# Transposed attention blocks through DRAM, keys permuted, and the product with v one point later

## The chip, the cores and the metric

The kernel runs on one core of a Trainium2 chip. A core has a matrix engine (TensorE; PE in the profile, with its weight loads shown apart as PEld), VectorE (DVE), ScalarE (ACT), GpSimd (POOL) and SyncE (SP), which here issues nearly all the DMAs. Each engine works through its own instructions in order; semaphores tie the engines and the DMAs together. The metric is the device time of one execution in microseconds: the median of three runs before was 1619.12 us (1618.91 to 1619.42). The profiled execution took 1619.76 us, of which the profile's span is 1618.0 us.

## The reference, cut to what matters

One layer of an encoder is computed for two sequences of 512 tokens, width 1024: a state-space branch, a differential attention, a cross attention to 256 memory tokens, a gated merge of the three, and a gated feed-forward network. The change touches the differential attention alone. It has 4 heads with two maps of 64 query and key columns each, and values 128 wide:

```
s = jnp.einsum('bqhd,bkhd->bhqk', qblk, k).astype(jnp.float32) * scale
probs = jax.nn.softmax(s, axis=-1).reshape(Bn, DIFF_HEADS, 2, Q_BLOCK, L)
w = probs[:, :, 0] - lam * probs[:, :, 1]
return jnp.einsum('bhqk,bkhe->bqhe', w.astype(v.dtype), v)
```

The sum over the keys in the last line does not depend on the order in which the keys are numbered, as long as w and v number them alike.

## The kernel before, in words

All large products are made in three passes: each float32 operand is split into a rounded part and a rest (`split`, lines 132 to 139: ScalarE copies the rounded part, line 134, and VectorE subtracts, line 135), and TensorE multiplies high by high, high by low and low by high. Weights arrive by DMA as `wf` (line 146) and are split to `wh` and `wl`. A projection (`units`) makes one output bank of 512 columns, `bkmm`, out of 24 products.

The differential attention runs over 16 pairs of query blocks: 4 heads, 2 sequences, 2 pairs of 128 queries. A pair u goes through five steps.

- `scores(2u)`: TensorE makes the score banks `bksc` of two query blocks (128 queries by 512 keys, two maps). VectorE takes the row maxima (line 858), ScalarE the exponentials (lines 861 and 862), VectorE the reciprocals and the combination of the two maps (lines 864 to 866), and VectorE transposes the result in blocks of 32 by 32 into the tile `eT` (line 867). `eT` has one buffer.
- The same function then issues 16 DMAs on SP's queue (line 872). Each takes 32 partitions of `eT` to 32 partitions of the tile `pL`, so that keys stand on the partitions and queries in the free dimension. One run of bytes in them is 64 floats.
- `turn(u)`: ScalarE copies the rounded part of `pL` into `pH`, VectorE puts the rest into `pL`. The two tiles come from one pool of four slots.
- `outputs(u)`: TensorE multiplies with the values, 12 products of 256 columns into the bank `bkoo` ("the product with v" below). After the second pair of a head and sequence ScalarE copies the bank out (line 899).
- `squares` and `normed`: the norm over the head, and a DMA of the result to DRAM (line 919), where the last of the three merges fetches it.

The values come from `v_units`, with x as the stationary operand (128 tokens by 128 columns, loaded into TensorE) and 256 weight columns moving over it: 384 such products in all, half of them during the cross attention and half during this stage. Keys and queries come from `qk_units`, through `rotated`.

Between these steps `fill` hands TensorE projections from a list (keys and queries of the next heads, values, gates, then the merges). A step of the loop has two such fillings. On TensorE the order written down is kept. On the other engines and on SP's queue a scheduler has ordered the instructions at build time, from estimated times.

Of the kernel before, what the change touches and what calls it, by code (L numbers as in the profile page):

```python
# [10 lines left out]
F32 = mybir.dt.float32  # L11
F32R = mybir.dt.float32r
# [7 lines left out]
P = 128  # L20
L = 512
DM = 1024
KD = DM // P
# [49 lines left out]
def encoder(ctx: ExitStack, tc: tile.TileContext, a, out):  # L73
# [14 lines left out]
    def open_tags(es, side=None, **tags):  # L88

        for tag, n in tags.items():  # L90
            pools[tag] = es.enter_context(tc.tile_pool(name=tag, bufs=n, side=side, reuse_waits="tile"))
# [14 lines left out]
    def slot(tag, shape=(P, NT), dt=F32, name="sl"):  # L106
        return pools[tag].tile(list(shape), dt, tag=tag, name=name)
# [23 lines left out]
    def split(hi, lo, src, scale=None):  # L131

        if scale is None:
            h = S.copy(hi, src)  # L134
            l_ = V.tensor_tensor(out=lo, in0=src, in1=hi.bitcast(F32), op=ALU.subtract)  # L135
        else:
            h = S.activation(out=hi, in_=src, func=AF.Copy, scale=scale)
            l_ = V.scalar_tensor_tensor(out=lo, in0=src, scalar=scale, in1=hi.bitcast(F32), op0=ALU.mult, op1=ALU.subtract)
        return h, l_
# [456 lines left out]
    def fill(n):  # L596
        nonlocal owed
        owed += n
        while owed > 0 and queue:
            r = next(queue[0], None)  # L600
            if r is None:
                queue.pop(0)
            else:
                owed -= r
        if not queue:
            owed = 0
# [28 lines left out]
    def v_units(hf, res):  # L635

        ws = [weight(a["w_v"][hf, c]) for c in range(2)]
        for s in range(NS):
            vh, vl = (slot("v2" if hf == 1 and s == 0 else "v", [P, 4, 256], F32R, n_) for n_ in ("vh", "vl"))
            for i2 in range(2):  # L640
                ob = bank()
                for kt in range(KD):
                    wh, wl = ws[kt // 4]
                    wsl = slice(kt % 4 * 256, kt % 4 * 256 + 256)
                    for i in range(2):
                        dst = ob[:, i * 256 : i * 256 + 256]
                        tk = slice(s * L + (2 * i2 + i) * P, s * L + (2 * i2 + i + 1) * P)
                        PE.matmul(dst, xh[kt][:, tk], wh[:, wsl], start=(kt == 0 and i == 0), stop=False)
                        PE.matmul(dst, xh[kt][:, tk], wl[:, wsl], start=False, stop=False)
                        PE.matmul(dst, xl[kt][:, tk], wh[:, wsl], start=False, stop=(kt == KD - 1 and i == 1))  # L650
                    if kt == KD - 1:
                        split(*(v_[:, 2 * i2 : 2 * i2 + 2, :].rearrange("p t n -> p (t n)") for v_ in (vh, vl)), ob)
                    if kt % 2 == 1:
                        yield 6
            res.append((vh, vl))
# [76 lines left out]


    open_banks(mm=2, sc=2, tr=1, oo=1)
    open_tags(phase, v2=2, qk=12, pT=4)
    aes = ExitStack()
    ap_ = aes.enter_context(tc.tile_pool(name="att", bufs=2, reuse_waits="tile"))
    acol = aes.enter_context(tc.tile_pool(name="acol", bufs=2, reuse_waits="tile"))
# [5 lines left out]
    def rotated(is_q):  # L744

        hl = tuple(slot("qk", [P, NT], F32R, n_) for n_ in ("rh", "rl"))

        def use(s, o):
            cs = slice(s * L, (s + 1) * L)
            t1 = ap_.tile([P, L], F32, tag="t1", name="t1", bufs=1)  # L750
            V.tensor_tensor(out=t1, in0=o, in1=rope[0], op=ALU.mult)
            t2 = ap_.tile([P, L], F32, tag="t2", name="t2", bufs=1)
            V.stream_shuffle(t2, o, mask)  # L753
            PO.tensor_tensor(out=t2, in0=t2, in1=rope[1], op=ALU.mult)  # L754
            PO.tensor_tensor(out=t1, in0=t1, in1=t2, op=ALU.add)
            split(hl[0][:, cs], hl[1][:, cs], t1, scale=0.125 if is_q else None)

        return hl, use

# [76 lines left out]
              gate_units(), merges()]  # L836
    s0, ss, osb = {}, {}, {}
    pl, ods = {}, {}

    def scores(i):  # L840
        nonlocal last_e
        h, s, qt = steps[i]
        cs = slice(s * L, (s + 1) * L)
        if h and s == qt == 0:
            finish(dk[h])
        if qt == 0:
            s0[h, s] = acol.tile([P, 4], F32, tag="s0", name="s0", bufs=3)
        (qh, ql), (kh, kl) = qk[h, True], qk[h, False]
        sc = [pools["sc"].tile([P, 2, L], F32, tag="sc", name="bksc") for _ in range(2)]
        for t in range(2):  # L850
            qs_ = slice(s * L + (qt + t) * P, s * L + (qt + t + 1) * P)
            for q_, k_ in ((qh, kh), (qh, kl), (ql, kh)):
                for mp, rows in enumerate(MAPS):
                    PE.matmul(sc[t][:, mp], q_[rows, qs_], k_[rows, cs], start=(k_ is kh and q_ is qh), stop=(q_ is ql))
        eT = ap_.tile([P, 16, 2, 32], F32, tag="eT", name="eT", bufs=1)
        for t in range(2):
            nb = acol.tile([P, 2], F32, tag="dnb", name="nb")
            V.tensor_reduce(out=nb, in_=sc[t], axis=AX.X, op=ALU.max, negate=True)
            e0, e1 = (ap_.tile([P, L], F32, tag=f"d{mp}e", name="e", bufs=2 - mp) for mp in range(2))
            sm0, sm1 = s0[h, s][:, qt + t : qt + t + 1], acol.tile([P, 1], F32, tag="ds", name="sm")  # L860
            S.activation(out=e0, in_=sc[t][:, 0], func=AF.Exp, bias=nb[:, 0:1], accum_out=sm0)
            last_x = S.activation(out=e1, in_=sc[t][:, 1], func=AF.Exp, bias=nb[:, 1:2], accum_out=sm1)
            r1 = acol.tile([P, 1], F32, tag="dr", name="r")
            V.reciprocal(r1, sm1)
            V.scalar_tensor_tensor(out=r1, in0=r1, scalar=nlam, in1=sm0, op0=ALU.mult, op1=ALU.mult)
            V.scalar_tensor_tensor(out=e0, in0=e1, scalar=r1, in1=e0, op0=ALU.mult, op1=ALU.add)
            last_e = last_x, V.transpose(eT[:, :, t, :], e0)
        raw = pl[i // 2] = slot("pT", [P, 4, 2 * P], F32R, "pL")
        rows = eT.rearrange("p (j c) t q -> p j c (t q)", c=4)
        for g in range(4):  # L870
            for c in range(4):
                nc.sync.dma_start(raw.bitcast(F32)[32 * c : 32 * c + 32, :, 64 * g : 64 * g + 64], rows[32 * g : 32 * g + 32, :, c])

    def turn(u):
        lo, hi = pl[u], slot("pT", [P, 4, 2 * P], F32R, "pH")
        split(hi, lo, lo.bitcast(F32))
        pT[u] = hi, lo

    def outputs(u):

        h, s, qt = steps[2 * u]
        if h == 2 and s == 0:
            finish(v1_)
        vh, vl = (v1 if h >= 2 else v0)[s]
        vs = slice((h % 2) * P, (h % 2) * P + P)
        pH, pL = pT.pop(u)
        if qt == 0:
            ods[h, s] = bank("oo")
            osb[h, s] = rp.tile([P, L], F32, tag="nsq", name="osb", bufs=2)
        cs = slice(qt * P, (qt + 2) * P)  # L890
        od = ods[h, s][:, cs]
        for j in range(4):
            PE.matmul(od, vh[:, j, vs], pH[:, j, :], start=(j == qt == 0), stop=False)
            PE.matmul(od, vh[:, j, vs], pL[:, j, :], start=False, stop=False)
            PE.matmul(od, vl[:, j, vs], pH[:, j, :], start=False, stop=(j == 3 and qt == 2))
        if qt == 2:
            for a_ in range(2):
                cs = slice(a_ * 2 * P, (a_ + 1) * 2 * P)
                S.copy(osb[h, s][:, cs].rearrange("p (t g q) -> p g t q", t=2, q=32),
                       ods[h, s][:, cs].rearrange("p (g t q) -> p g t q", t=2, q=32))  # L900
# [18 lines left out]
        nc.sync.dma_start(bD[1, h, :, s * L : (s + 1) * L], osb[h, s])  # L919

    n, first = len(steps), {}
    for i in range(-1, n + 3):
        if i % 2 and i + 1 < n:
            scores(i + 1)
        fill(10 if i < n - 1 else 16)
        if i % 2 and 0 < i <= n:
            turn(i // 2)
        fill(10)
        if i % 2 == 0 and 0 < i <= n:
            outputs(i // 2 - 1)  # L930
        if 1 < i <= n + 1 and steps[i - 2][2] == 3:
            squares(i - 2)
        if i > 2 and steps[i - 3][2] == 3:
            normed(i - 3)
        if i in (17, 19, 21, 23):
            t = (0, 1, 3, 2)[(i - 17) // 2]
            with yielding(last_e):
                merge_split(b0, 0, t, "v" if t == 3 else "qk", first[t])
        if i in (15, 17, 19, 21):
            t = (0, 1, 3, 2)[(i - 15) // 2]  # L940
            first[t] = merge_load(0, t)
# [927 lines left out]
```

## Time and profile before

| | |
|---|---|
| median of three runs | 1619.12 us (1618.91 to 1619.42) |
| profiled execution | 1619.76 us, span 1618.0 us |
| TensorE busy | 1575.7 us, 97% of the span |
| VectorE, ScalarE, GpSimd busy | 74%, 39%, 34% |
| TensorE busy from 519 to 783 us (differential attention) | 233.62 of 264 us, granted clock 0.94 |

The profile's busy time of TensorE includes time in which it works at a lower clock: a row's PEclk says which share of full speed was granted. Matrix products overlap in the records: one of 512 columns is shown as 0.39 us long, while the next one starts 0.23 us after it. Idle time is therefore counted only from the shown end of the one before.

### The profile page before, as it was taken

Reading aid. Unit: us, or ns where it says so; the run is one execution under the profiler, and the core shown is the slowest. Engines: PE = TensorE matmul, PEld = TensorE weight load, DVE = VectorE, ACT = ScalarE, POOL = GpSimd, SP = SyncE. Lnnn points to the kernel's source line nnn. Section 1 sums busy time; section 2 is a strip of 40 time slices with the busy share of each in tenths; the row PEclk is TensorE's granted clock in tenths of the full one; section 3 lists DMA queues with packets and bytes.
Section 4 is the critical chain, followed back from the end, with each engine's and each line's share of the span. In section 5 each row is a group of like instructions: output and inputs, shape, how many; then the busy total and the mean of one; then the engine's idle time right before and its main releaser. Section 6 shows DMA issues by size and latency. Waiting matters only on the chain. (4 is left out here: it accounts for less than half of the span.)

```text
span 1618.0 us, 21693 instructions
## 1 busy us (share of the span) xinstructions
PE 1575.7 (97%) x7706; PEld 1312.5 (81%) x7706; DVE 1190.4 (74%) x1843; ACT 632.8 (39%) x1107; POOL 552.2 (34%) x434
## 2 busy tenths in 40 slices
PE   9999999999999899888999999999999999999998
PEld 7888888888898678677788888888888888888877
DVE  7978994076764777767545659888898887988874
ACT  6544223175552346455223444233333323323323
POOL 0010000001322211210144344777677554435673
PEclk9999999999999999999999999999999999999999
DMA  9554533685762232235653542323333223785512
GB/s 356 188 165 141 174 118 124 188 279 186 249 227 85 57 120 56 77 96 183 215 177 104 161 139 65 115 95 124 130 117 121 108 92 127 287 313 197 169 59 105
DMA packets 142540, 246.26 MB, mean 152 GB/s; under 512 B 50528, under 2 KB 82272, under 8 KB 142432
## 3 DMA queue, kind: packets, MB, share of 16 engines
q1 hardware_dynamic: 141856, 244.46, 45.3%
q8 instruction: 61, 1.00, 0.3%
q14 instruction: 47, 0.39, 0.1%
q10 hardware_dynamic: 576, 0.41, 0.1%
HBM read 165.16 MB, written 71.27 MB: 146 GB/s over the span
## 5 line engine op out<-in xcount | busy, mean ns | idle before, releaser
L66 PE MATMUL bkmm<-xh,wh 128*128 128x512 f32 x640 | 253.3, 396 | 0.0
L66 PE MATMUL bkmm<-xh,wl 128*128 128x512 f32 x640 | 250.4, 391 | 0.0
L66 PE MATMUL bkmm<-xl,wh 128*128 128x512 f32 x640 | 249.9, 391 | 0.0
L66 PE MATMUL bkmm<-tl,wh 128*128 128x512 f32 (+1 forms) x621 | 241.1, 388 | 0.0
L66 PE MATMUL bkmm<-th,wl 128*128 128x512 f32 (+1 forms) x621 | 240.7, 388 | 0.0
L66 PE MATMUL bkmm<-th,wh 128*128 128x512 f32 (+1 forms) x621 | 240.7, 388 | 0.0
L134 ACT CAST wh<-wf 128x1024 fp32r<-128x1024 f32 (+2 forms) x134 | 117.5, 877 | 259.6 <-PE bkmm L66 174.0
L135 DVE TENSOR_TENSOR wl<-wf,wh 128x1024 fp32r<-128x1024 f32 (+2 forms) x134 | 148.3, 1106 | 62.5 <-ACT wh L134 57.8
L66 PEld LDWEIGHTS bkmm<-xh,wh 128*128 128x128 f32 x640 | 120.3, 188 | 27.5 <-issue 4.4
L66 PE MATMUL bkmm<-th,w 128*128 128x512 f32 x432 | 140.6, 391 | 1.8 <-DVE nsq L1128 1.2
L66 PEld LDWEIGHTS bkmm<-xh,wl 128*128 128x128 f32 x640 | 120.2, 188 | 25.7 <-issue 0.4
L66 PEld LDWEIGHTS bkmm<-xl,wh 128*128 128x128 f32 x640 | 120.3, 188 | 22.9
L66 PEld LDWEIGHTS bkmm<-th,wh 128*128 128x128 f32 x621 | 116.6, 188 | 24.0
L66 PEld LDWEIGHTS bkmm<-tl,wh 128*128 128x128 f32 x621 | 116.6, 188 | 24.0
L66 PEld LDWEIGHTS bkmm<-th,wl 128*128 128x128 f32 x621 | 116.5, 188 | 23.9 <-DVE wl L135 0.2
L1191 POOL TENSOR_TENSOR up<-up,acc 128x512 f32<-128x512 f32 x44 | 83.7, 1920 | 90.5 <-DVE up L1128 86.8
L452 POOL TENSOR_TENSOR raw<-raw 128x128 f32<-128x128 f32 x28 | 14.7, 524 | 288.8 <-DVE nb L543 231.9
L66 PEld LDWEIGHTS bkmm<-th,w 128*128 128x128 f32 x432 | 80.9, 188 | 21.9 <-DVE nsq L1128 2.1
L793 POOL TENSOR_TENSOR mg<-mg,gl 128x1024 f32<-128x1024 f32 x16 | 43.8, 2737 | 145.8 <-DVE gl L789 141.1
L66 PE MATMUL bkmm<-tl,w 128*128 128x512 f32 x216 | 84.1, 389 | 0.0
L134 ACT CAST wh<-ws 128x1024 fp32r<-128x1024 f32 x44 | 46.3, 1053 | 89.2 <-PE bkmm L66 58.0
L754 POOL TENSOR_TENSOR t<-t,rs 128x512 f32<-128x512 f32 x16 | 26.3, 1645 | 160.1 <-DVE t L753 111.2
(661 smaller groups left out, 3596.5 us busy)
## 6 DMA issues: line engine op xcount, KB each, us to landing
wf<-in_w_in SPq DMA_DIRECT2D x40, 512.0 KB, 3.9
wD<-hl SPq DMA_DIRECT2D x28, 512.0 KB, 2.9
w<-wD SPq DMA_DIRECT2D x28, 512.0 KB, 4.8
gD<-gt SPq DMA_DIRECT2D x24, 512.0 KB, 3.0
gl<-gD SPq DMA_DIRECT2D x24, 512.0 KB, 4.1
wf<-in_w_fg SPq DMA_DIRECT2D x22, 512.0 KB, 3.5
wf<-in_w_fu SPq DMA_DIRECT2D x22, 512.0 KB, 3.5
aD<-ac SPq DMA_DIRECT2D x22, 512.0 KB, 2.8
```

Of the source, the lines that this page charges most:

```text
L66: return self.put(self.eng.matmul(*args, **kw))
L134: h = S.copy(hi, src)
L135: l_ = V.tensor_tensor(out=lo, in0=src, in1=hi.bitcast(F32), op=ALU.subtract)
L452: PO.tensor_tensor(out=a22, in0=a21, in1=a22, op=ALU.add)
L754: PO.tensor_tensor(out=t2, in0=t2, in1=rope[1], op=ALU.mult)
L793: PO.tensor_tensor(out=mg[m], in0=mg[m], in1=gt, op=ALU.add)
L1191: PO.tensor_tensor(out=up, in0=up, in1=accs[s], op=ALU.mult)
```

## The change

The 16 DMAs of a pair are replaced by four stores of 32 partitions each from `eT` to a DRAM tile `eD`, and one load of 128 partitions from there to `pL`. One run of bytes is now 256 floats. In `eD`, and so in `pL`, a partition holds every fourth key of a block of 128. Two other places are numbered to match: `rotated` writes the split keys with the columns of each block of 128 permuted (it reads its source at a step of four floats), and `v_units` takes as its stationary operand every fourth token, a step of four floats, in place of 128 tokens side by side. `turn` and `outputs` see `pL` and `pH` in the arrangement that the load leaves. `pL` gets three slots and `pH` one, in place of four for both. In the loop, `outputs(u)` moves from the end of one step to after the first filling of the next, ahead of the `turn` of the pair after it; `squares` and `normed` move back by one step too. No arithmetic is added or removed.

```diff
@@ v_units
-                        tk = slice(s * L + (2 * i2 + i) * P, s * L + (2 * i2 + i + 1) * P)
-                        PE.matmul(dst, xh[kt][:, tk], wh[:, wsl], start=(kt == 0 and i == 0), stop=False)
-                        PE.matmul(dst, xh[kt][:, tk], wl[:, wsl], start=False, stop=False)
-                        PE.matmul(dst, xl[kt][:, tk], wh[:, wsl], start=False, stop=(kt == KD - 1 and i == 1))
+                        xh_, xl_ = (x_[kt][:, s * L + 2 * i2 + i : (s + 1) * L : 4] for x_ in (xh, xl))
+                        PE.matmul(dst, xh_, wh[:, wsl], start=(kt == 0 and i == 0), stop=False)
+                        PE.matmul(dst, xh_, wl[:, wsl], start=False, stop=False)
+                        PE.matmul(dst, xl_, wh[:, wsl], start=False, stop=(kt == KD - 1 and i == 1))
@@
-    open_tags(phase, v2=2, qk=12, pT=4)
+    open_tags(phase, v2=2, qk=12, pL=3, pH=1)
@@ rotated
-            split(hl[0][:, cs], hl[1][:, cs], t1, scale=0.125 if is_q else None)
+            if is_q:
+                split(hl[0][:, cs], hl[1][:, cs], t1, scale=0.125)
+            else:
+                split(*(t_[:, cs].rearrange("p (c j k) -> p c j k", c=4, j=4) for t_ in hl), t1.rearrange("p (c k j) -> p c j k", c=4, j=4))
@@
+    eD = drp.tile([16, 4, 4, 32, 2 * P], F32, name="eD")
@@ scores
-        raw = pl[i // 2] = slot("pT", [P, 4, 2 * P], F32R, "pL")
-        rows = eT.rearrange("p (j c) t q -> p j c (t q)", c=4)
         for g in range(4):
-            for c in range(4):
-                nc.sync.dma_start(raw.bitcast(F32)[32 * c : 32 * c + 32, :, 64 * g : 64 * g + 64], rows[32 * g : 32 * g + 32, :, c])
+            nc.sync.dma_start(eD[i // 2, g].rearrange("c k n -> k c n"),
+                              eT[32 * g : 32 * g + 32].rearrange("k (c j) t q -> k c (j t q)", c=4))
+        pl[i // 2] = slot("pL", [P, 4, 2 * P], F32R, "pL")
+        nc.sync.dma_start(pl[i // 2].bitcast(F32), eD[i // 2].rearrange("g c k n -> (c k) g n"))
@@ turn
-        lo, hi = pl[u], slot("pT", [P, 4, 2 * P], F32R, "pH")
+        lo, hi = pl[u], slot("pH", [P, 4, 2 * P], F32R, "pH")
         split(hi, lo, lo.bitcast(F32))
-        pT[u] = hi, lo
+        pT[u] = tuple(t_.rearrange("p g (j n) -> p j g n", j=4) for t_ in (hi, lo))
@@ the loop over the steps
-    for i in range(-1, n + 3):
+    for i in range(-1, n + 4):
         if i % 2 and i + 1 < n:
             scores(i + 1)
         fill(10 if i < n - 1 else 16)
+        if i % 2 and 2 < i <= n + 1:
+            outputs(i // 2 - 1)
         if i % 2 and 0 < i <= n:
             turn(i // 2)
         fill(10)
-        if i % 2 == 0 and 0 < i <= n:
-            outputs(i // 2 - 1)
-        if 1 < i <= n + 1 and steps[i - 2][2] == 3:
-            squares(i - 2)
-        if i > 2 and steps[i - 3][2] == 3:
-            normed(i - 3)
+        if 2 < i <= n + 2 and steps[i - 3][2] == 3:
+            squares(i - 3)
+        if i > 3 and steps[i - 4][2] == 3:
+            normed(i - 4)
```

How the order moves is seen best on two engines. On SP's queue, in the middle of the stage, where the last projections of keys and queries load their weights (`wf<-in_w_in`), stood before:

```order
L872 DMA pL<-eT 32x4x64 x16
L919 DMA bD<-osb 128x512
L146 DMA wf<-in_w_in 128x1024
L872 DMA pL<-eT 32x4x64 x32
L919 DMA bD<-osb 128x512
L146 DMA wf<-in_w_in 128x1024 x2
L872 DMA pL<-eT 32x4x64 x32
L919 DMA bD<-osb 128x512
L146 DMA wf<-in_w_up 128x512
```

At the same place now stands (lines 872 to 876 are the new DMAs, and line 919 has become 923):

```order
L873 DMA eD<-eT 32x4x256 x4
L923 DMA bD<-osb 128x512
L876 DMA pL<-eD 128x4x256
L873 DMA eD<-eT 32x4x256 x4
L876 DMA pL<-eD 128x4x256
L146 DMA wf<-in_w_in 128x1024
L923 DMA bD<-osb 128x512
L146 DMA wf<-in_w_in 128x1024
L873 DMA eD<-eT 32x4x256 x4
L876 DMA pL<-eD 128x4x256
```

A pair has five DMAs on the queue in place of 16, and one of them, the load, waits for the four stores ahead of it; a weight load can stand right behind it.

On TensorE, at the first product with v, stood before (`bkoo` is the product's bank, `bksc` that of the scores, which `x2` marks as two products on halves of the rows):

```order
L66 MATMUL bkoo<-pH,vh 128x256
L66 MATMUL bkoo<-pL,vh 128x256
L66 MATMUL bkoo<-pH,vl 128x256
L66 MATMUL bksc<-rh 128x512 x2
L66 MATMUL bksc<-rl,rh 128x512 x2
L66 MATMUL bksc<-rh,rl 128x512 x2
```

and now:

```order
L66 MATMUL bksc<-rh,rl 128x512 x2
L66 MATMUL bkmm<-xh_127,wh 128x512
L66 MATMUL bkmm<-xl_135,wh 128x512
L66 MATMUL bkmm<-xh_127,wl 128x512
L66 MATMUL bkmm<-xh_128,wh 128x512
L66 MATMUL bkmm<-xl_136,wh 128x512
L66 MATMUL bkmm<-xh_128,wl 128x512
L66 MATMUL bkoo<-pH,vh 128x256
L66 MATMUL bkoo<-pL,vh 128x256
L66 MATMUL bkoo<-pH,vl 128x256
```

The product has moved behind the next pair's scores and one filling of 6 (elsewhere 12) projections.

## The prediction

> **What bounds the kernel now.** First the page's busy shares, then the span cut into stretches, since a mean over the whole says little.
>
> ```profile
> span 1618.0 us, 21693 instructions
> PE 1575.7 (97%) x7706; PEld 1312.5 (81%) x7706; DVE 1190.4 (74%) x1843; ACT 632.8 (39%) x1107; POOL 552.2 (34%) x434
> ...
> 519.00:783.00 264.00, 233.62 (x1236) 191.06 (x1234) 188.48 (x297) 127.80 (x285) 39.14 (x24) 0.94 0.35 107
> 783.00:1618.00 835.00, 825.75 (x3754) 684.88 (x3752) 635.55 (x746) 269.79 (x378) 461.24 (x324) 1.00 0.42 142
> ```
>
> TensorE is the bound. The columns of the last two rows are PE, PEld, DVE, ACT, POOL, granted clock, DMA share and GB/s. Nearly all that TensorE loses it loses between 519 and 783 us, the differential attention: 264 − 233.6 = 30.4 us idle, and a granted clock of 0.94. What it waits for there, from the view of waits (us in total, times, longest):
>
> ```profile
> PE bkoo L66 <- DMA pL<-eT: 12.4, 3, 4.7
> PE bkoo L66 <- DVE pL L135: 11.5, 6, 4.2
> PE bkoo L66 <- DMA wf<-in_w_v: 2.7, 1, 2.7
> PE bkoo L66 <- ACT pH L134: 2.0, 3, 1.0
> PE bkmm L66 <- ACT wh L134: 1.9, 2, 1.4
> PE bkoo L66 <- DMA bD<-osb: 0.4, 1, 0.4
> ```
>
> Five of the six rows are the product with v (`bkoo`): 12.4 + 11.5 + 2.7 + 2.0 + 0.4 = 29.0 us in 14 waits. All of them are one lateness, that of a pair's transposed block on its way from `eT` to `pL` and `pH`. The waits also cost clock. I laid windows on the six stretches at half clock; the first of them and their sum:
>
> ```profile
> 546.80:550.21 3.41, 3.28 (x15) 2.96 (x17) 0.23 (x2) 0.62 (x1) 2.49 (x2) 0.50 0.20 48
> ...
> sum 30.70, PE 25.79 PEld 21.18 DVE 12.01 ACT 6.55 POOL 11.51; mean PE 4.30 PEld 3.53 DVE 2.00 ACT 1.09 POOL 1.92
> ```
>
> Work that lasted 25.8 us at half clock would last half of that. Each of the six stretches follows one of the long waits, of about 3 us or more; the short ones left the clock at 1.00. [...]
>
> Why the block is late is seen in one pair, followed through the timelines of TensorE, VectorE, SP and ScalarE:
>
> ```profile
> 628.59 0.40 PE L66 MATMUL bksc<-rh,rl 64*128 64x512 f32 x2
> ...
> 633.65 0.75 DVE L866 SCALAR_TENSOR_TENSOR e<-e,r 128x512 f32<-128x512 f32 x1
> ...
> 636.97 1.30 DVE L867 STREAM_TRANSPOSE eT<-e 128x512 f32<-128x512 f32 x2 [2.50 <-DMA pL<-eT]
> ...
> 624.13 25.38 SPq L872 DMA_DIRECT2D pL<-eT  x32
> ...
> 650.97 1.05 ACT L134 CAST pH<-pL 128x1024 fp32r<-128x1024 f32 x1 [2.50 <-DMA pL<-eT]
> ...
> 655.90 1.21 DVE L135 TENSOR_TENSOR pL<-pL,pH 128x1024 fp32r<-128x1024 f32 x1
> ...
> 652.07 0.38 PE L66 MATMUL bkoo<-pH,vh 128*128 128x256 f32 x1 [0.39 <-DMA bD<-osb]
> 657.17 0.58 PE L66 MATMUL bkoo<-pL,vh 128*128 128x256 f32 x1 [4.72 <-DMA pL<-eT]
> ```
>
> The scores end at 629.0. VectorE has the combined block at 634.4, then waits 2.5 us for `eT`, because SP is still issuing the DMAs of the pair before: 32 of them, two pairs, back to back for 25.4 us, 0.79 us each, 12.7 us a pair. The data land 21.9 us after the scores, `pL` is finished 28.1 us after them, and the product, which TensorE reached at 652, waits until 657.17. SP's issue time is thus as long as a pair's whole work on TensorE, and the lateness passes from pair to pair.
>
> **The change part by part.**
>
> *TensorE's distance.* Products in the order follow each other at steps that these rows give:
>
> ```profile
> 509.81 0.39 PE L66 MATMUL bkmm<-xl,wh 128*128 128x512 f32 x1
> 518.88 0.39 PE L66 MATMUL bkmm<-xh,wl 128*128 128x512 f32 x1
> ...
> 779.60 0.28 PE L66 MATMUL bkoo<-pH,vh 128*128 128x256 f32 x1
> 780.91 0.28 PE L66 MATMUL bkoo<-pH,vl 128*128 128x256 f32 x1
> ...
> 788.46 0.60 PE L69 MATMUL bktr<-ident,osb 128*128 128x128 f32 x4
> 788.82 0.49 PE L66 MATMUL bkmm<-yh,wh 128*128 128x512 f32 x1
> ```
>
> That is 0.227 us for 512 columns (40 steps in 9.07 us), 0.119 for 256 (11 in 1.31), 0.09 for 128 (4 in 0.36). With these, two score products side by side taken as one of 512 columns, the built orders hold between a pair's last score and its product with v 21.6 us of TensorE work on the mean before (20.4 to 23.9), and 26.6 now (23.2 to 28.1). The move alone gives 5 us of room.
>
> *The way of the block.* The nearest rows for the new DMAs, issue in ns (least, median, most) and time to landing in us:
>
> ```profile
> L872 SPq DMA_DIRECT2D pL<-eT x256: 585/599/1843, 529.3 to 772.9; - x128
> L1690 SPq DMA_DIRECT2D u__1192<-uD x32: 303/429/1443, 74.8 to 118.0; - x32
> ...
> pL<-eT SPq DMA_DIRECT2D x256, 32.0 KB, 1.9
> gl<-gD SPq DMA_DIRECT2D x24, 512.0 KB, 4.1
> fb<-aD SPq DMA_DIRECT2D x9, 512.0 KB, 5.9
> bD<-osb SPq DMA_DIRECT2D x8, 256.0 KB, 2.5
> ```
>
> A store has 32 x 4 runs like the old DMA, so 0.6 us of issue, four in 2.4 us; SP then waits for the last landing, 1.9 (small DMAs) to 2.5 us (`bD`, a store to DRAM); the load issues in 0.4 to 0.8 us and lands in 4.1 to 5.9. From block to `pL` that is 2.4 + 2.2 + 0.5 + 4.5 = 9.6 us (8.8 to 11.6), against 16 x 0.79 + 1.9 = 14.5 before. SP is held 5 to 6 us a pair, not 12.7, and behind the waiting load stand at most a weight load and the next pair's stores. `eT` is free again after the stores, 4.6 us after its last write, so VectorE's wait for it goes.
>
> Now the pair: scores end at 0, combined block at 5.4, transposes to 6.7, landing at 16.3. `pH` has one buffer, so its cast waits for the product of the pair before, which by the same count ends 9.9 to 11.8 us ahead of this pair's own, so about 16 us after these scores; it is no later than the landing. The cast and the subtraction:
>
> ```profile
> L134 ACT CAST pH<-pL x16: 1030/1048/1087, 541.8 to 775.0; 128x1024 fp32r<-128x1024 f32 x16
> L135 DVE TENSOR_TENSOR pL<-pL,pH x16: 1204/1218/2286, 545.7 to 776.1; 128x1024 fp32r<-128x1024 f32 x16
> ```
>
> They end at 16.3 + 1.0 + 1.2 = 18.5 with free engines, at 23.5 if the subtraction stands 5 us behind other VectorE work as it did at 655.9. TensorE wants it at 26.6. So the waits go, with 3 to 8 us to spare.
>
> *The sum.* Idle −29.0. Each wait is counted from the modelled end of the product before, 0.39 − 0.227 = 0.16 us too late: 14 x 0.16 = −2.3. Clock −25.79/2 = −12.9. Together −44.2. What stays: the small waits (1.9 for `wh`) are not touched; I add +3 for new short ones (two or three of the 1.0 to 1.4 us kind that the rows of `pH` and `wh` show, below what costs clock).
>
> *Strided reads.* The values' stationary operand is now read at a step of 16 bytes, 384 loads. No load in this trace is strided. The row of the load, and two products at half clock:
>
> ```profile
> L66 PEld LDWEIGHTS bkmm<-wl,xh 128*128 128x128 f32 x128 | 24.5, 192 | 0.0
> ...
> 657.55 0.41 PE L66 MATMUL bkoo<-pH,vl 128*128 128x256 f32 x1
> 657.76 0.41 PE L66 MATMUL bkoo<-pH,vh 128*128 128x256 f32 x1
> ```
>
> Loads run under the products (0.19 us long, a step of 0.12). Below, the strided load stays under them: 0; a gain is excluded, since the products stay. Above, all of a load shows: 384 x 0.19 = 73 us. In between, at half pace: the step at half clock is 0.21, so at most 384 x 0.09 = 36 us; and since products of 128 columns step at 0.09, a load fits into 0.09, doubled 0.18, 0.06 more than 0.119: 23 us. I take 0, because the load has 0.119 us where 0.09 is enough at full pace. [...] The keys' split reads at the same step, 8 casts and 8 subtractions of about 0.65 us; doubled, 5 us on each of two engines that are not the bound: 0.
>
> The predicted profiled time is 1619.76 − 44.2 + 3 = 1578.6; that execution lay 0.6 above the median, so **1578 us**.
>
> **The rivals.** (a) *VectorE takes over as the bound* of the stage. For: 188.5 us busy, and waits of its own that the change leaves:
>
> ```profile
> DVE r L864 <- ACT e L862: 10.3, 24, 0.9
> DVE rl L138 <- ACT rh L137: 10.2, 4, 3.7
> DVE wl L135 <- ACT wh L134: 6.1, 5, 4.2
> ```
>
> 188.5 + 26.6 = 215 us, against a stage of 264 − 44 = 220; a subtraction that now blocks VectorE for `pL` about 1 us a pair would make it 231, and 11 us of the gain go: 1590. Against: elsewhere TensorE runs full beside a VectorE at 76% over 835 us. (b) *The strided load at half pace*: 1578 + 23 = 1601, at most 1614. (c) *The strided load shows in full*: 73 − 44 + 3 makes it slower, 1651; it turns slower from 44/384 = 0.115 us a load on. Against: loads overlap products everywhere in this trace. (d) *The change doesn't shorten the wait*, since store, receipt and load together take as long as the old queue: this needs 5 us more than the bounds; 1617.
>
> **How the numbers follow.** Forecast (1572 to 1585) 0.60, (a) 0.18, (b) 0.11, (c) 0.05, (d) 0.06. The range of 1572 to 1604 holds the forecast, (a) and most of (b), over 8 in 10. Faster by over 0.2% (3 us, about what a measurement here can tell): 0.60 + 0.18 + 0.11 = 0.89; (d) splits into 0.04 same and 0.02 slower; slower 0.07.
>
> **What would show it.** Right: between 519 and about 739 us a granted clock of 1.00, no wait of `bkoo` beyond 1 us, four stores and a load taking 5 to 6 us of SP a pair, no VectorE wait for `eT`. Wrong: steps of the values' products above 0.119 us (b, c), waits of `bkmm` for VectorE (a), `bkoo` still waiting for `pL` (d).

## The result and the profile after

The change made the kernel slower: 1631.63 us (median of four runs, 1628.81 to 1632.09) against 1619.27 us before, a ratio of 1.0068 (95% interval 1.0051 to 1.0086). The forecast was 1578, in a range of 1572 to 1604. The profiled execution, the shortest of the four, took 1628.81 us, 9.05 more than the profiled one of before; the medians differ by 12.4.

First the busy shares, then the stretch of the differential attention (columns: PE, PEld, DVE, ACT, POOL, granted clock, DMA share, GB/s).

```profile
span 1627.0 us, 21422 instructions
...
PE 1608.2 (99%) x7706; PEld 1347.2 (83%) x7706; DVE 1198.3 (74%) x1843; ACT 634.6 (39%) x1107; POOL 547.6 (34%) x434
...
519.00:783.00 264.00, 257.71 (x1287) 214.59 (x1286) 196.98 (x305) 132.40 (x287) 47.21 (x30) 0.99 0.43 136
```

Between 519 and 783 us TensorE is idle for 6.3 us where it was for 30.4, and its clock is 0.99 instead of 0.94. Yet the kernel is slower, with TensorE busy for 1608.2 us where it was 1575.7 for the same 7706 products. So the time went into the products themselves. The view of waits of the kernel after:

```profile
PE bkmm L66 <- DVE mg L792: 3.5, 2, 3.1
...
PE bkmm L66 <- ACT gt L630: 1.1, 2, 0.8
...
PE bkmm L66 <- DVE gl L792: 0.9, 1, 0.9
PE bkoo L66 <- DVE pL L135: 0.8, 1, 0.8
```

The product with v (`bkoo`) waits 0.8 us, once; it was 29.0 us in 14 waits. One half-clock stretch is left of six. It begins at 755.2, during the 3.1 us wait for `mg`, a merge's bank that VectorE had not emptied; a window on it:

```profile
755.00:762.00 7.00, 5.69 (x14) 4.08 (x16) 5.98 (x11) 2.13 (x5) 0.00 (x0) 0.51 0.63 222
```

What became slower stands in the group of the values' weight loads (`v_units`; busy time, then mean ns) and in the timeline of TensorE in the cross attention:

```profile
L66 PEld LDWEIGHTS bkmm<-wl,xh 128*128 128x128 f32 x128 | 42.1, 329 | 0.6 <-DVE wl L135 0.6
```

```profile
437.71 0.39 PE L66 MATMUL bkmm<-wl,xh 128*128 128x256 f32 x1
...
440.05 0.39 PE L66 MATMUL bkmm<-wh,xl 128*128 128x256 f32 x1
```

A load with the 16-byte step is recorded with 0.329 us instead of 0.192, and the products follow each other every 2.34/10 = 0.234 us, not every 0.12. That is 0.114 us more for each of 384 products, 43.8 us, and more than the change gains elsewhere. Taken over all 384 products of the two traces, from the start of each to the start of the next, it is 91.4 us against 47.0 before: 44.5 more. The clock was 1.00 there, so it is not a half-clock stretch, although the step is close to the one at half clock (0.21).

The block's way through DRAM is shorter than predicted. One pair, from the timelines of VectorE and SP, and the row of landing times (the last figure, in us):

```profile
621.39 0.71 DVE L871 STREAM_TRANSPOSE eT<-e 128x512 f32<-128x512 f32 x1
...
622.13 1.77 SPq L873 DMA_DIRECT2D eD<-eT  x4
...
625.78 0.38 SPq L876 DMA_DIRECT2D pL<-eD  x1
```

```profile
pL<-eD SPq DMA_DIRECT2D x16, 512.0 KB, 4.0
```

Four stores in 1.77 us, 1.9 us until the load is issued (it waits for the last store's landing), the load's issue 0.38 us and its landing 4.0 us: 8.0 us, where the prediction counted 9.6. SP is held 4 us a pair.

### The profile page after: what moved, and what is told of

Its sections match the earlier page's. It is cut to its first block, busy times and chain, and to the rows that moved or that the text cites. A ratio compares the mean times of both kernels' runs of the same rounds, so it can differ in the third digit from the quotient of the medians.

```text
span 1627.0 us, 21422 instructions
## 1 busy us (share of the span) xinstructions
PE 1608.2 (99%) x7706; PEld 1347.2 (83%) x7706; DVE 1198.3 (74%) x1843; ACT 634.6 (39%) x1107; POOL 547.6 (34%) x434
## 5 line engine op out<-in xcount | busy, mean ns | idle before, releaser
L452 POOL TENSOR_TENSOR raw<-raw 128x128 f32<-128x128 f32 x28 | 14.6, 522 | 311.6 <-DVE nb L543 231.8
L66 PE MATMUL bkmm<-yh,wh 128*128 128x512 f32 x192 | 77.0, 401 | 4.6 <-DVE mg L792 3.5
```

What stands on the lines that cost most here:

```text
L66: return self.put(self.eng.matmul(*args, **kw))
L452: PO.tensor_tensor(out=a22, in0=a21, in1=a22, op=ALU.add)
```

## The experiments

The theory: the way through DRAM and the later product do what they should, and the strided loads of the values' stationary operand alone give the gain back. The main rival: the gain was never there, because the new way brings waits of its own, which the slow products only cover.

**1. The change with values read contiguously.** The keys may stand in any order if the values stand in the same. In the change a partition of `pL` holds four keys that stand side by side (not every fourth key, as the part on the change puts it), and the 128 keys of one product are every fourth of the sequence's 512. Here the 128 keys of one product stand side by side, so that the values are read as before, and the keys' split reads its source in runs of 32. The diff is shortened:

```diff
-    xh_, xl_ = (x_[kt][:, s * L + 2 * i2 + i : (s + 1) * L : 4] for x_ in (xh, xl))
+    tk = slice(s * L + (2 * i2 + i) * P, s * L + (2 * i2 + i + 1) * P)      # xh[kt][:, tk], xl[kt][:, tk]
-    split(*(t_[:, cs].rearrange("p (c j k) -> p c j k", ...) for t_ in hl), t1.rearrange("p (c k j) -> p c j k", c=4, j=4))
+    split(*(t_[:, cs].rearrange("p (c j k) -> p c j k", ...) for t_ in hl), t1.rearrange("p (j c k) -> p c j k", c=4, j=4))
```

> The change with another numbering of keys: the values' stationary operand is read contiguously again, as before the change, and the keys' split reads runs of 32 instead of a step of 4 words; DMAs, buffers and order are the change's. Theory (the stride alone ate the gain; 384 loads x 0.114 us = 43.8 us): 1578 to 1588 us, the step of the values' products back at 0.119 us, their load records back at about 0.19 us. Rival 1 (the way through DRAM or the later product costs what it saves, the slow loads only sit where TensorE would wait anyway): 1615 us or more, with waits of the product with v or half-clock stretches coming back as the values' products get short. Rival 2 (VectorE becomes the bound once the loads are fast, (a) of the prediction): about 1590.

Measured: 1590.87 us (1589.47 to 1594.11) against 1618.62, ratio 0.9833 (0.9817 to 0.9848). On every engine and on SP's queue the order of instructions in the trace is that of the change, so the difference to the change, 40.8 us, belongs to the way of reading alone. Groups of the values' weight load and of the keys' split in this kernel, and seven steps of the values' products:

```profile
L66 PEld LDWEIGHTS bkmm<-wl,xh 128*128 128x128 f32 x128 | 25.3, 197 | 2.6 <-DVE wl L135 2.6
...
L134 ACT CAST rh<-t 128x512 fp32r<-128x512 f32 x8 | 5.0, 619 | 26.9 <-POOL t L755 26.9
...
L135 DVE TENSOR_TENSOR rl<-t,rh 128x512 fp32r<-128x512 f32 x8 | 5.4, 672 | 6.7 <-ACT rh L134 6.7
...
437.76 0.28 PE L66 MATMUL bkmm<-wl,xh 128*128 128x256 f32 x1
...
438.60 0.28 PE L66 MATMUL bkmm<-wh,xl 128*128 128x256 f32 x1
```

The load is back at 0.197 us and the step at 0.84/7 = 0.120. The theory holds against rival 1: 43.8 us were expected from the loads, 40.8 came back, and no wait of the product with v returned. But 1590.9 is above the theory's 1578 to 1588 and on rival 2's number. The waits of this kernel show what is missing:

```profile
PE bkmm L66 <- DVE mg L792: 6.2, 3, 2.9
PE bkmm L66 <- DVE wl L135: 2.4, 1, 2.4
PE bkmm L66 <- ACT gt L630: 1.6, 2, 1.1
...
PE bkmm L66 <- DVE gl L792: 0.8, 1, 0.8
...
PE bkoo L66 <- DVE pL L135: 0.5, 1, 0.5
```

**2. The stride alone, in the kernel before.** The diff is the first hunk of the change and nothing else.

> The kernel before with one part of the change alone: the values' stationary operand read at a step of 4 words (the values are then numbered otherwise than the keys, so the product with v is not the reference's; its work is the same). Theory: half of the 384 loads lie in the cross attention, where TensorE hardly waits, 192 x 0.114 = 22 us in full; the other half lies in the differential attention, whose waits can hide between nothing and all of it: 1641 to 1663 us. Rival 1 (the loads cost nothing of their own): 1619. The step of the values' products is 0.233 us by the theory, 0.119 by the rival.

Measured: 1662.01 us against 1618.62, ratio 1.0272 (1.0255 to 1.029): 43.4 us more, the upper end of the theory. Loads are recorded with 0.326 to 0.329 us. The waits of the product with v did not give way:

```profile
L66 PE MATMUL bkoo<-pL,vh 128*128 128x256 f32 x64 | 22.5, 352 | 25.1 <-DVE pL L135 15.3 <-DMA pL<-eT 9.0 <-DMA gl<-gD 0.9
...
L66 PE MATMUL bkoo<-pH,vh 128*128 128x256 f32 x64 | 20.9, 326 | 2.7 <-ACT pH L134 2.7
```

25.1 + 2.7 = 27.8 us, before 29.0. In the timeline of before, 149 of the second half's 192 products of the values run between 620 and 645 us, and the product with v does not wait once in that stretch. There was nothing there to hide behind, which fits, though no run tests it apart.

**3, 4 and 5. Other strides.** The change with one line altered: a step of 2, 8 or 3 words instead of 4.

```diff
-    x_[kt][:, s * L + 2 * i2 + i : (s + 1) * L : 4]
+    x_[kt][:, s * L + i : s * L + i + 2 * P : 2]       # step 2
+    x_[kt][:, 4 * i2 + i : NT : 8]                     # step 8
+    x_[kt][:, s * L + i : s * L + i + 3 * P : 3]       # step 3
```

> The change with the values' stationary operand at a step of 2 words (8 bytes) instead of 4 (it then takes other tokens' values than the product needs). [...] Rival 1 (any stride slows the load alike): as the change, 0.233 us and 1629 to 1632. Rival 2 (the pace falls with the bytes that are spanned): between, about 0.16 to 0.18 us and 1595 to 1610.

> The change with the values' stationary operand at a step of 8 words (32 bytes) instead of 4 (other tokens' values than the product needs). [...] Rival (the price grows with the bytes that are spanned): more than 0.233 us, 1640 us or more.

> The change with the values' stationary operand at a step of 3 words (12 bytes; other tokens' values than the product needs). [...]

The first and the last of a run of the values' products, from the timelines of the kernels with step 2, 3 and 8:

```profile
437.85 0.28 PE L66 MATMUL bkmm<-wl,xh 128*128 128x256 f32 x1
...
439.05 0.28 PE L66 MATMUL bkmm<-wh,xl 128*128 128x256 f32 x1
```

```profile
437.88 0.34 PE L66 MATMUL bkmm<-wh,xh 128*128 128x256 f32 x1
...
439.29 0.34 PE L66 MATMUL bkmm<-wh,xl 128*128 128x256 f32 x1
```

```profile
438.04 0.41 PE L66 MATMUL bkmm<-wh,xh 128*128 128x256 f32 x1
...
439.98 0.40 PE L66 MATMUL bkmm<-wh,xl 128*128 128x256 f32 x1
```

These are 10, 8 and 8 steps. With the first experiment (step 1) and the change (step 4):

| step in words | us from product to product | time, us | ratio to before |
|---|---|---|---|
| 1 | 0.120 | 1590.87 | 0.9833 (0.9817 to 0.9848) |
| 2 | 0.120 | 1594.32 | 0.9851 (0.9834 to 0.9867) |
| 3 | 0.176 | 1610.20 | 0.9945 (0.9928 to 0.9962) |
| 4 | 0.234 | 1631.63 | 1.0068 (1.0051 to 1.0086) |
| 8 | 0.242 | 1633.85 | 1.0094 (1.0078 to 1.0110) |

0.176/3 and 0.234/4 are both 0.059 us for each word of the step. At that price a step of 2 would need 0.117 us (an estimate from these two points), just under the product's own 0.12, and would be hidden, as the row of step 2 shows. From 4 to 8 words the price hardly grows: it is 0.008 us more, 1633.85 us instead of 1631.63. My estimates before these runs were 0.119 us and 1578 to 1588 us at a step of 2, 0.175 us (three quarters of 0.233) and 1610 to 1615 us at 3, and 0.233 us and 1629 to 1632 us at 8. The steps of the products are met within 0.009 us, so "any stride" (0.233 us at a step of 2) and "the bytes that are spanned" (0.16 to 0.18 at 2, 1640 us or more at 8) fall. The time at step 8 is 2 us over the estimate and far from the rival's 1640; at step 2 it is 6 us over, but the products keep the full pace. What the trace of step 2 has beside that: waits for `mg` of 5.4 us and for `wl` of 2.3, much as in experiment 1, three half-clock stretches of 3.41 us (experiment 1 has one before the tail), and the keys' split still at a step of 16 bytes.

**6. Does a slow load hide under a longer product?** The kernel of experiment 1, with a step of 4 words in the stationary weights of 18 projections:

```diff
-    ws = slice(k * P, (k + 1) * P)
+    ws = slice(k // 4 * 4 * P + k % 4, (k // 4 + 1) * 4 * P, 4) if st else slice(k * P, (k + 1) * P)   # st: 8 slices of weights
```

> The first experiment's kernel (values contiguous again, 1590.9 us) with a step of 4 words in other loads: the stationary weights of 18 projections of queries, keys and gates (8 slices each, so 18 x 2 x 8 x 3 = 864 loads), whose moving operand is 512 columns long and whose products follow each other every 0.227 us; the weights are then others than the reference's, the work is the same. Theory (load and product overlap, and the longer of the two sets the step: 0.233 us against 0.227): at most 864 x 0.006 = 5 us more, 1590 to 1598 us. Rival (what a strided load takes longer comes on top of the product, 0.114 us each): 864 x 0.114 = 98 us more, about 1689 us.

Measured: 1599.79 us (1595.79 to 1600.36) against 1618.76, ratio 0.987 (0.9852 to 0.9889), 8.9 us over experiment 1. That is slightly over the theory's range and nowhere near the rival's 1689. From the timeline of TensorE:

```profile
527.95 0.63 PE L66 MATMUL bkmm<-xh,wh 128*128 128x512 f32 x1
528.42 0.40 PE L66 MATMUL bkmm<-xl,wh 128*128 128x512 f32 x1
528.67 0.40 PE L66 MATMUL bkmm<-xh,wl 128*128 128x512 f32 x1
...
530.77 0.40 PE L66 MATMUL bkmm<-xh,wl 128*128 128x512 f32 x1
```

The last two are 9 steps in 2.10 us, 0.233 each: the load's pace, since the product would need 0.227. So load and product overlap, and the longer of the two sets the step. The first row, behind the score products, shows where the rest lies: the first product of a run took 0.47 us to the next one. Counted over the two traces, 65 of the 864 products stand first in a run, and their steps add up to 25.4 us against 18.0 in experiment 1, 0.115 each: there the surplus of the load shows in full. The other 799 take 190.3 us against 184.9, 0.007 each. Together that is 12.9 us more; waits are a little shorter than in experiment 1 (4.9 us for `mg` instead of 6.2), and there is one half-clock stretch more, so that the 8.9 are met only roughly.

**7. The wait that was left.** In experiment 1 TensorE waits for `mg`. One such place, from the timelines of SP, ScalarE, VectorE and TensorE:

```profile
704.52 1.83 SPq L873 DMA_DIRECT2D eD<-eT  x4
...
709.39 0.37 SPq L876 DMA_DIRECT2D pL<-eD  x1
...
714.37 1.04 ACT L134 CAST pH<-pL 128x1024 fp32r<-128x1024 f32 x1 [2.97 <-DMA pL<-eD]
...
715.32 0.68 ACT L866 ACTIVATE e<-bksc,nb 128x512 f32<-128x512 f32 x1
...
715.45 1.23 DVE L135 TENSOR_TENSOR pL<-pL,pH 128x1024 fp32r<-128x1024 f32 x1 [2.73 <-ACT pH L134]
...
716.59 0.68 DVE L792 SCALAR_TENSOR_TENSOR mg<-gl,bkmm 128x512 f32<-128x512 f32 x1
...
717.33 0.50 PE L66 MATMUL bkmm<-yh,wh 128*128 128x512 f32 x1 [2.86 <-DVE mg L792]
```

The load landed 9.85 us after the first store. ScalarE stood before it with the cast, ahead of the last exponential; VectorE stood behind the cast; and the emptying of the merge's bank, for which TensorE waited, stood behind the subtraction. The block itself was needed only later. The edit queues the cast and the subtraction behind the last exponential and the last transpose of the next pair:

```diff
         if i % 2 and 0 < i <= n:
-            turn(i // 2)
+            with yielding(last_e):
+                turn(i // 2)
```

> The first experiment's kernel (contiguous values, keys in runs of 32), with one thing more: the cast to pH and the subtraction to pL are queued behind the last exponential and the last transpose of the next pair on ScalarE and VectorE, not wherever the scheduler put them. In the first experiment's trace ScalarE waited 2.97 us for a landing in front of the last exponential (714.37), VectorE 2.73 us for that cast, and behind it stood the emptying of a merge's bank, for which TensorE waited 2.86 us; a second such place is at 734.58. Theory (the gain still missing, 1590.9 against 1578, is this wait in the queues, not VectorE's load): TensorE's waits for mg fall from 6.2 us to 2 us or less, 1583 to 1588 us. Rival (VectorE is simply full, (a) of the prediction): the waits move elsewhere and the time stays at 1589 to 1593.

Measured: 1585.12 us (1584.94 to 1585.46) against 1619.40, ratio 0.9791 (0.9776 to 0.9805), the fastest kernel of this study. Waits of TensorE:

```profile
PE bkoo L66 <- DVE pL L135: 2.6, 2, 1.6
PE bkmm L66 <- DVE mg L792: 2.0, 2, 1.7
PE bktr L69 <- DVE rs L199: 2.0, 2, 1.3
PE bkmm L66 <- ACT gt L630: 1.5, 1, 1.5
PE bkmm L66 <- DVE wl L135: 1.5, 1, 1.5
```

The waits for `mg` fall from 6.2 to 2.0 us, as the theory said, the longest wait is 1.7 us, and no half-clock stretch is left before the tail. A part comes back as a wait for `pL` (2.6). VectorE has the same work as in experiment 1 (205.2 and 205.4 us busy from 519 to 783), so it was its queue's order, not its load. What stands between 1585 and 1578 lies in part in these five rows, 9.6 us in all against the 1.9 + 3 that the prediction left; no run takes the rest apart.

**8. The two parts apart.** The way through DRAM alone (experiment 1 with the product with v at its old place), and the move alone (the kernel before, its 16 DMAs a pair, product one point later):

```diff
# the way through DRAM alone, against experiment 1
-        if i % 2 and 2 < i <= n + 1:
-            outputs(i // 2 - 1)
...
+        if i % 2 == 0 and 0 < i <= n:
+            outputs(i // 2 - 1)
# the move alone, against the kernel before: the same lines the other way round, and
-    open_tags(phase, v2=2, qk=12, pT=4)
+    open_tags(phase, v2=2, qk=12, pL=3, pH=1)
```

> The way through DRAM alone: the first experiment's kernel with the product with v (and the norm behind it) at its place of before. The block is finished 18.5 to 23.5 us after the scores by the prediction's count, and TensorE wants it after 21.6. Theory (both parts work, and the way of the block is most of it): waits of the product with v of some 3 to 8 us instead of 29, 1593 to 1605 us. Rival (the way through DRAM is no shorter, (d) of the prediction): 1612 us or more. Other rival (the move adds nothing): as the first experiment, 1589 to 1593.

> The move alone: the kernel before, with its 16 DMAs a pair and its keys in order, but the product with v and the norm one point later (three buffers for pL, one for pH, as in the change). The room grows by 5 us, while the 16 issues still hold SP 12.7 us a pair. Theory (the lateness is mostly SP's issue time): half of the 29 us of waits stay, 1600 to 1612 us. Rival (5 us of room are enough, and the way through DRAM was not needed): 1589 to 1595 us. Other rival (the lateness passes from pair to pair, and the move gains nothing): 1616 us or more.

Measured: the way through DRAM alone 1609.25 us (1608.28 to 1610.17), ratio 0.9939 (0.9925 to 0.9954); the move alone 1604.82 (1600.19 to 1605.64), ratio 0.9906 (0.9889 to 0.9923); both against 1619.40. The second is where the theory had it; 10.7 us of the product's waits stay, where half of 29 were expected. The first is 4 us slower than its range. Waits of TensorE, VectorE and ScalarE with the way through DRAM alone, the last two in the stage only:

```profile
PE bktr L69 <- DVE rs L199: 10.7, 5, 5.9
PE bkoo L66 <- DVE pL L135: 5.0, 6, 1.0
...
PE bkoo L66 <- ACT pH L134: 3.3, 2, 2.5
...
DVE pL L135 <- ACT pH L134: 28.5, 11, 5.5
...
ACT pH L134 <- DMA pL<-eD: 42.3, 14, 7.5
```

The product with v itself waits 5.0 + 3.3 us, close to the expected 3 to 8. But 14 of 16 casts now wait on ScalarE for their landing, 42.3 us in all, VectorE waits behind them, and the norm's small operation `rs`, which stands behind both, makes TensorE's transposes wait 10.7 us; granted clock 0.96. My expectation had counted the block's way only, not what stands behind it. The parts alone gain 10.2 and 14.6 us, together 27.8 (experiment 1).

## Why the prediction was wrong

Its own sign of being wrong came: the values' products step at 0.234 us, above 0.119. Its signs of being right came too (clock 1.00 from 519 to 739 us, no wait of `bkoo` beyond 1 us, no wait of VectorE for `eT`). Step by step:

- **Waits of the product with v, −29.0**: right. 29.0 fell to 0.8 us, to 0.5 with the loads at full pace.
- **Modelled ends, −2.3**: 14 counted waits became one; the term itself cannot be measured apart.
- **Clock, −12.9**: nearly. One stretch is left, with 5.69 us of work at half clock, which costs 2.8; −10.1.
- **New short waits, +3**: right in size with the change (3.5 + 1.1 + 0.9 less the 1.9 for `wh`, 3.6), but by luck, since most of it is one wait of 3.1 us for `mg`, with half clock behind it, and not two or three of 1.0 to 1.4 us; too small with fast loads: 6.2 + 2.4 + 1.6 + 0.8 is 11.0, less 1.9 is 9.1, and the wait of 2.4 brought a half-clock stretch, 1.7 us more. I had looked for waits of TensorE for the block, and asked what waits behind the block on VectorE only in rival (a).
- **The way of the block**: right. 8.0 us in the ordinary pair, 9.85 in a slow one, against 9.6; SP held 4 us a pair, not 5 to 6.
- **The keys' split doubled, 5 us on each of two engines, hidden**: right in kind. Casts took 8.9 us instead of 5.0, subtractions 8.6 instead of 5.4 (rows below and in experiment 1), off the path.

```profile
L134 ACT CAST rh<-t 128x512 fp32r<-128x512 f32 x8 | 8.9, 1118 | 27.5 <-POOL t L755 27.5
...
L135 DVE TENSOR_TENSOR rl<-t,rh 128x512 fp32r<-128x512 f32 x8 | 8.6, 1072 | 7.7 <-ACT rh L134 7.7
```

- **Strided reads, 0: the step that failed.** "I take 0, because the load has 0.119 us where 0.09 is enough at full pace." The 0.09 came from contiguous loads; at a step of 4 words the load needs 0.234, twice the product, and the surplus is on TensorE's path 384 times: +43.8 us. My bound in between (0.21, 36 us) came from a row of the half clock, which says nothing of a strided read; only the upper bound, 73 us, held. No rival had it whole: (b) had the load set the pace, but at 36 us at most, and (c) had it on top of the product, while experiment 6 shows the two overlapping and the longer one setting the step. That the cost of 0.114 us a load lies at the break-even of 0.115 that (c) names is chance: by the other terms as measured the gain is 37.0 us, and 0.096 us a load was enough to lose it. The "half pace" behind (b) was my estimate, for which no row gave a reason, and no run shows it: experiments 3 to 5 and the change have 0.120 us at a step of 2 words, 0.176 at 3, 0.234 at 4 and 0.242 at 8.

The sum with measured terms: −28.2 − 2.3 + 3.6 − 10.1 + 43.8 = +6.8 us, or +7.5 with the 44.5 counted over all 384 products; the profiled executions differ by +9.05. The other 1.5 to 2.2 us I cannot assign.

Rival (a) put 1590 on VectorE. Experiment 1 gives that time, but experiment 7 shows that it was a place in two queues: moving the cast and the subtraction gained 5.8 us without taking any work from VectorE. The rest, from 1585 to 1578, stays open. Rival (d) is ruled out by experiment 8: alone, the way through DRAM gains 10.2 us.

## What to carry to other kernels

An operation that the trace has never seen, on the engine that bounds and hundreds of times, must not be priced at the lower bound: 384 times 0.114 us was more than the whole gain. When data are renumbered, let the stride fall on the operand whose reads have slack, or renumber in runs: runs of 32 did here what a step of 4 words did, with the cast at 0.62 us instead of 1.12 and the values' step at 0.120 instead of 0.234. And an operation that waits for a DMA in an in-order queue should stand as late as its consumer allows; what is queued behind it waits as well (queueing the cast and the subtraction later gained 5.8 us in experiment 7).

## What the runs showed of the hardware that I had not expected

- The stationary operand's load set the step of the products at 0.176 us when read at a step of 3 words, 0.234 at 4 and 0.242 at 8, and was free under a product of 256 columns up to two words of step (0.120 us at step 1 and 2). Under 512 columns (0.227 us) a step of 4 words cost 0.007 us a product, and 0.115 for the first product of a run.
- A step of 4 words also slowed ScalarE's cast of 128x512 from 0.62 to 1.12 us and VectorE's subtraction from 0.67 to 1.07 us.
- The length of a wait alone did not decide whether it cost clock; where it fell did. In experiment 1, the wait of 2.43 us that ended at 603.35 was followed by half clock, and that of 2.86 us that ended at 717.33 was not. In every trace of this study the half-clock stretches lie on a grid of 3.41 us and last one or two windows of it. The first wait lies in one window of that grid, of which TensorE works 0.84 us; the second is cut by a border, and 1.82 and 2.15 us of work are left in its two windows:

```profile
600.00:603.41 3.41, 0.84 (x6) 0.44 (x4) 3.31 (x7) 1.52 (x9) 1.08 (x1) 1.00 0.57 154
...
712.64:716.05 3.41, 1.82 (x10) 1.21 (x8) 0.68 (x2) 1.68 (x4) 0.00 (x0) 1.00 0.09 30
716.05:719.47 3.42, 2.15 (x9) 1.80 (x10) 3.42 (x7) 1.51 (x3) 0.00 (x0) 1.00 0.34 92
```

Over the eleven traces, from 20 to 1570 us, 30 windows at full clock were followed by half clock, and all had 1.71 us or more without work; of those that were not, none had more than 1.75. So the border lay at about half of the 3.41 us here, and a wait of 1.79 us was enough (the move alone, at 611.33). In the kernel before, 686.75 to 690.16 us had 1.73 us without work and half clock after it, and 744.78 to 748.19 us had 1.69 and full clock after it. In the tail, after 1570 us, 0.7 to 2.2 us were enough. The prediction's "about 3 us or more" was a wrong reading: in the kernel before, half clock also followed the wait of 2.67 us that ended at 563.57.
